# A two-layer encoder on one core: matmul operands and tiles moved to other places in SBUF, modulo 512 bytes

## The chip, the core and the metric

The kernel runs on one core of one Trainium2 chip. The metric is the device time in microseconds (us) of the whole program; the time before is the median of three runs. Everything is float32; products are taken as three matmuls on halves (see below), so the work of TensorE (PE) is three times that of the plain products.

## The reference, cut to what matters

512 tokens of width 1024 pass through two layers. Layer 0 mixes by stick-breaking attention, layer 1 by a gated linear recurrence (RG-LRU); each is followed by an MLP with squared ReLU, and a last norm ends it.

```
x = x + stick_breaking_attention(rms_norm(x, norm_mix[0]), w_qkv, w_o)
u = relu(rms_norm(x, norm_mlp[0]) @ mlp_w1[0]);  x = x + (u * u) @ mlp_w2[0]
x = x + rglru_block(rms_norm(x, norm_mix[1]), ...)
u = relu(rms_norm(x, norm_mlp[1]) @ mlp_w1[1]);  x = x + (u * u) @ mlp_w2[1]
return rms_norm(x, norm_final)
```

## The kernel before

**Halves.** Each float32 operand is split into a high half that PE reads as fp32r and a low half that is the rest. ScalarE (ACT) writes the high half with a copy, VectorE (DVE) the low one with a subtraction. A product takes three matmuls: high by high, high by low, low by high (`three`, L219 to L221; `up`, L966; `times`, L1061). x lies in `xgh` and `xgl`, a second pair of activations in `bh` and `bl`, the weights in `wh` and `wl`, of which `wpool` holds four pairs of 4 KB per partition, and in the RG stage `wmore` two more.

**A matmul has two operands in SBUF.** The stationary one (128 columns, 512 bytes per partition) is loaded ahead of the matmul (the profile's PEld rows), the moving one (512, 384, 256 or 128 columns) streams through. All rows of a tile that a matmul reads start a multiple of 512 bytes from the tile's start, so the distance between the two operands' starts, modulo 512, is fixed by where the tiles start.

**Stages in order of time.** Attention with its projections and output product to about 250 us; the first quarter of the MLP's up-projection ("m1", `Mlp.squared`, L219 to L221, 512 columns) to 294.9; layer 0's MLP to 564; the RG block with its output product to about 715; m1 of layer 1 to 763.8; layer 1's MLP to the end.

**The MLP** (`Mlp.run`, L1061 and L966) takes the rest as Strassen-like seven-product schemes (`PRODUCTS`): "up" passes with two units of seven steps, 24 matmuls of 256 columns each (x's blocks moving, weights stationary), and "down" passes with 14 steps, 12 matmuls of 512 columns each (the weights moving, the blocks of u stationary: `bh`, `bl` for unit 0, `sh`, `sl` for unit 1). In up, products P1, P2 and P4 read `xgh` and `xgl`; P5 and P3 read the tile `s41` with `low`; P6 reads a corner of `bh` or `bl` with `low`; P7 reads `xgh` with `low`. Each layer has four down passes and three up passes between them. The order of a down pass stands in `ORDERS`; "mid" is P1 0, P5 0, P1 1, P2 0, P5 1, P6 0, P6 1, P3 0, P3 1, P7 0, P7 1, P2 1, P4 0, P4 1, where the digit is the unit.

**What sets the order.** PE's instructions are in written order. Within `Mlp.run` those of DVE and ACT are too (`Ordered`): `leave(i)` runs when step i is written, evacuates its PSUM bank, and prepares the weights of step i + 4 (`operand`: ACT copies `wh`, then DVE writes `wl`), for which the pair of step i has to be free. Sums of weight blocks are added by DVE (`b<-b,b`) or by DMAs that accumulate (POOL's queue).

**Places.** Tiles of a pool lie one behind the other in the order in which they are first asked for, and pools lie one behind the other in the order in which they are opened; so whatever is put ahead of a tile, or lengthens one, moves all that is placed behind it.

Of the kernel before, what the change touches and what calls it, by code (L numbers as in the profile page):

```python
# [11 lines left out]
F32 = mybir.dt.float32  # L12
F32R = mybir.dt.float32r
AF = mybir.ActivationFunctionType
# [3 lines left out]
P = 128  # L18
S = 512
D = 1024  # L20
C = D // P
# [3 lines left out]
EPS = 1e-6  # L25
RG_C = 8.0
SCALE = HD ** -0.5


START = [  # L30
# [31 lines left out]
def hybrid_encoder(  # L62
# [24 lines left out]
    V, A, G, PE = nc.vector, nc.scalar, nc.gpsimd, nc.tensor  # L87

    const = ctx.enter_context(tc.tile_pool(name="const", bufs=1))
# [13 lines left out]
    def f(ap):  # L103
        return ap.bitcast(F32)


    colt = const.tile([P, cols.shape[1]], F32, tag="colt", name="colt")

    def col(name):
        o, n = COLS[name]  # L110
        return colt[:, o : o + n]
# [4 lines left out]
    make_identity(nc, ident)  # L116
    eps_t = const.tile([P, 1], F32, tag="eps", name="eps_t")
    V.memset(eps_t, EPS)

    xgh = const.tile([P, C, S], F32R, tag="xgh", name="xgh")  # L120
    xgl = const.tile([P, C, S], F32R, tag="xgl", name="xgl")
    bh = const.tile([P, C, S], F32R, tag="bh", name="bh")
    bl = const.tile([P, C, S], F32R, tag="bl", name="bl")

# [1 line left out]
    def halves(gname, c, xc):  # L126

        g = col(gname)[:, c : c + 1]
        A.activation(xgh[:, c, :], xc, AF.Identity, scale=g)
        return V.scalar_tensor_tensor(  # L130
            xgl[:, c, :], xc, g, f(xgh[:, c, :]), ALU.mult, ALU.subtract
        )
# [90 lines left out]
    def dense(src, ah, al, tag=None, halves=None, ks=range(C), ps=None):  # L223

        wh, wl = halves or slab(src, ks=ks)
        ps = bank(tag) if ps is None else ps
        for k in ks:
            three(ps, ah[:, k, :], al[:, k, :], wh[:, k, :], wl[:, k, :], k == ks[0], k == ks[-1])
        return ps

    def beside(ws, ah, al, pss, at, ks=range(C)):
# [8 lines left out]
    ctx.enter_context(tc.manual_schedule(engines={mybir.EngineType.PE}))  # L240


    lams = {
        n: const.tile([P, C], F32, tag=f"lam_{n}", name=n)
        for n in ("ab", "pp", "den", "s1", "s2", "pl", "c8", "c4")
    }
    c8, c4 = lams["c8"], lams["c4"]

    def softplus():

        ab, pp, den, s1, s2, pl, _, _ = lams.values()
        lam = col("lam")

        sigmoid = yield
        V.tensor_scalar(ab, lam, -1.0, None, ALU.mult)
        V.tensor_tensor(ab, ab, lam, ALU.max)
        with tc.issue_after(sigmoid.ins):
            A.activation(pp, ab, AF.Sigmoid, scale=-1.0)
        with tc.issue_after((yield).ins):
            V.tensor_scalar(den, pp, -1.0, 2.0, ALU.mult, ALU.add)  # L260
        V.reciprocal(den, den)
        V.tensor_tensor(s1, pp, den, ALU.mult)
        V.tensor_tensor(s2, s1, s1, ALU.mult)
        V.tensor_scalar(pl, s2, 1.0 / 17, 1.0 / 15, ALU.mult, ALU.add)
        for n in (13, 11, 9, 7, 5, 3, 1):
            V.tensor_tensor(pl, pl, s2, ALU.mult)
            V.tensor_scalar(pl, pl, 1.0 / n, None, ALU.add)
        V.tensor_tensor(pl, pl, s1, ALU.mult)
        V.tensor_scalar(den, lam, -1.0, 0.0, ALU.mult, ALU.max)
        V.scalar_tensor_tensor(c8, pl, 2.0, den, ALU.mult, ALU.add)  # L270
        V.tensor_scalar(c4, c8, RG_C * 0.5, None, ALU.mult)
        V.tensor_scalar(c8, c8, -RG_C, None, ALU.mult)
        yield
# [5 lines left out]
    NB = S // P  # L279
    PAIRS = H // 2  # L280
    half = [slice(0, HD), slice(HD, P)]
    so, early = {}, {}
# [4 lines left out]
    def home_tile(tag, n, name):  # L287
        return home.tile([P, S], F32, tag=tag, name=name, bufs=n)

    with ExitStack() as actx:  # L290
        hp = actx.enter_context(tc.tile_pool(name="hp", bufs=2))
        sp = actx.enter_context(tc.tile_pool(name="sp", bufs=1))


        later = sp.tile([P, S], F32, tag="later", name="later")
        G.memset(later, 0.0)
        G.affine_select(
# [11 lines left out]
        for i in range(2):  # L309
            both = []  # L310
            for nm in ("h", "l"):
                t = sp.tile([P, 2 * P], F32R, tag=f"last{nm}{i}", name=f"last{nm}{i}")
                G.memset(f(t[:, :P]), 0.0)
                both.append(t)
            lasts.append(both)
# [117 lines left out]
        def inverse():  # L433
# [9 lines left out]
            with tc.high_priority():  # L443
                norm["root"] = A.activation(rc, pc[:, :NB], AF.Sqrt, bias=eps_t, scale=1.0 / D)
                V.reciprocal(rc, rc)
                for t in range(NB):
                    ts = slice(t * P, (t + 1) * P)
                    V.tensor_scalar(diag[:, ts], ident, rc[:, t : t + 1], None, ALU.mult)
                V.tensor_scalar(rp, rc, SCALE, None, ALU.mult)
                V.tensor_scalar(rn, rc, -SCALE, None, ALU.mult)  # L450
            norm.update(rc=rc, rp=rp, rn=rn)
# [280 lines left out]
    def add_x(c, ps):  # L732
        V.tensor_tensor(x[c], x[c], ps, ALU.add)

    def residual(srcs, gname, begun={}, ready={}):

        for c in range(C):
            add_x(c, begun[c][0] if c in begun else dense(srcs[c], bh, bl, halves=ready.get(c)))
            halves(gname, c, x[c])

    residual(w_so, "mlp0", so, so_next)


# [23 lines left out]
    class Mlp:  # L767
# [28 lines left out]
        def __init__(self, ctx, layer):  # L796
            self.layer, self.sq, self.first = layer, Squares(), None
            self.V, self.A = Ordered(V), Ordered(A)
            self.mp = ctx.enter_context(tc.tile_pool(name=f"mlp{layer}", bufs=2))
            self.c = [  # L800
                self.mp.tile([P, 2, S], F32, tag=f"c{i}", name=f"c{i}", bufs=1) for i in range(4)
            ]
            self.begun, self.a = set(), {}
            self.turns = count()
            self.blocks = ExitStack()
            self.bp = self.blocks.enter_context(tc.tile_pool(name=f"blocks{layer}", bufs=2))
            self.u, self.lows, self.s3, self.slots = {}, {}, [], None

            self.s41 = self.bp.tile([P, C // 2, S], F32R, tag="s41", name="s41", bufs=1)

        def y(self, t, h):

# [500 lines left out]
    with ExitStack() as mctx:  # L1313
        mlp = Mlp(mctx, 0)

        dram = mctx.enter_context(tc.tile_pool(name="dram", bufs=1, space=bass.MemoryType.DRAM))
        away = dram.tile([P, C, S], F32, tag="away", name="away")
        squares = Squares()
        last = {}

        def feature(c, tag):

            pt = bank(tag)
            for t in range(NB):
                PE.transpose(
                    pt[:, t * P : (t + 1) * P], mlp.y(t, c // 4)[:, c % 4 * P : (c % 4 + 1) * P],
                    ident,
                )
            add_x(c, pt)
            last["low"] = halves("mix1", c, x[c])  # L1330

        def end(ws, xs):
            for i in range(2):
                for g in range(2):
                    mlp.times("P4", g, i, ws[g], xs[i], False)
                mlp.collect("P4", i, xs[i])
                if i == 0:
                    for c in range(4, C):
                        feature(c, "zzoo"[c - 4])
                        squares.chunk(c, x[c], e=G)  # L1340

        def between(c):
            nc.sync.dma_start(out=away[:, c, :], in_=x[c])
            if c == C - 1:
                soft.send(mlp.ready)

        def back():
            for c in range(C):
                x[c] = home_tile(*HOMES[c], "x")
                nc.sync.dma_start(out=x[c], in_=away[:, c, :])  # L1350

        end.ready = back
        mlp.quarters(between, end)

        begin = [bank("acc") for _ in range(2)]
        beside(
            [slab(w_in[C + i]) for i in range(2)], xgh, xgl, begin,
            {
                1: lambda: [feature(c, "z") for c in range(2)],
                2: lambda: [feature(c, "o") for c in range(2, 4)],  # L1360
            },
            (*range(4, C), *range(4)),
        )
        behind[0] = last["low"].ins
        third = slab(w_in[C + 2])
        behind[0] = None
        sq = squares
        with tc.tile_pool(name="squares", bufs=4) as pool:
            for c in range(4):
                sq.chunk(c, x[c], last["low"], pool)  # L1370

    wctx = ExitStack()

    wmore = wctx.enter_context(tc.tile_pool(name="wmore", bufs=2))


    with ExitStack() as rctx:
# [196 lines left out]
        for k in range(C):  # L1574
            for c in range(4):
                ps, wh, wl = begun[c]
                three(ps, bh[:, k, :], bl[:, k, :], wh[:, k, :], wl[:, k, :], k == 0, k == C - 1)

    residual(w_ro, "mlp1", begun, {4: ws["o4"]})
    wctx.close()  # L1580


    with ExitStack() as mctx:
        lp = mctx.enter_context(tc.tile_pool(name="last", bufs=1))
        mlp = Mlp(mctx, 1)

        def between(c):
# [20 lines left out]
                )  # L1608


        A.activation(lp.tile([P, 1], F32, tag="rt", name="early"), eps_t, AF.Sqrt)

        ss = lp.tile([P, NB, 3], F32, tag="ss", name="ss")
        bias = lp.tile([P, NB], F32, tag="bias", name="bias")

        def square(t, h, i, cols=slice(0, S), end=False):

# [129 lines left out]
```

## Time and profile before

| what | value |
|---|---|
| time, median of 3 runs | 1049.12 us (1048.78 to 1049.46) |
| span of the profiled execution | 1047.9 us; the median lies 1.2 us above it |
| PE matmul busy | 1035.1 us, 99% of the span, 5868 matmuls |
| DVE, ACT, POOL busy | 863.1 (82%), 701.5 (67%), 179.2 (17%) us |
| DMA | 159.41 MB, mean 152 GB/s |

The profile is of one execution. Matmuls are pipelined: a row's own length (0.28 us for 256 columns) is longer than the time until the next one starts. What a matmul costs is therefore read from start to start, or from a piece of the chain of work that counts them (24 in 2.88 us). "Idle before <-releaser" in a row is how long the engine stood still ahead of it, and what ended that. Steps are named by their product (P1 to P7) and unit, as above.

### The profile page before, as it was taken

The page shows a single profiled execution, that of the slowest core. Times are in us where ns is not written, and L with a number is a line of the kernel's source. Part 1 is how long each engine was busy: PE and PEld are TensorE (multiplying, and loading weights), DVE is VectorE, ACT ScalarE, POOL GpSimd, SP SyncE. Part 2 cuts the span into 40 slices and gives each one's busy share as a digit, 9 for nine tenths or more (in the row PEclk, how much of TensorE's full clock was granted, in tenths as well). Part 3 has the DMA queues.
Part 4 walks back from the last instruction along what each step waited for, and adds up shares of the span by engine and source line. Part 5 has one row for each costly group of instructions (what it writes and reads, how often), then busy time and mean ns, then how long its engine had stood idle before and what let it go on. Part 6 is the DMA issues. An engine that isn't in the chain of part 4 may idle for free.

```text
span 1047.9 us, 15859 instructions
## 1 busy us (share of the span) xinstructions
PE 1035.1 (99%) x5868; PEld 902.8 (86%) x5868; DVE 863.1 (82%) x1147; ACT 701.5 (67%) x1082; POOL 179.2 (17%) x238
## 2 busy tenths in 40 slices
PE   8999999999999999999999999999999999999997
PEld 7888888888888988988988788888888988988986
DVE  7888787848788898898899799984789797897897
ACT  6767676836766773773775699964755773773775
POOL 2344344420000010010011121200000010010013
PEclk9999999999999999999999999999999999999999
DMA  6745354537536667567582483352345667567553
GB/s 225 204 137 141 101 149 104 153 109 274 149 80 190 181 139 204 165 140 207 164 208 81 109 214 112 91 221 93 88 86 173 174 142 206 158 139 204 145 125 101
DMA packets 52828, 159.41 MB, mean 152 GB/s; under 512 B 6672, under 2 KB 7952, under 8 KB 52752
## 3 DMA queue, kind: packets, MB, share of 16 engines
q1 hardware_dynamic: 41808, 120.13, 34.4%
q0 software_dynamic: 10368, 37.75, 20.9%
q8 instruction: 46, 0.75, 0.3%
q10 hardware_dynamic: 576, 0.52, 0.2%
q14 instruction: 30, 0.25, 0.1%
HBM read 137.41 MB, written 4.19 MB: 135 GB/s over the span
## 4 chain that ended last, share of the span: by engine, by line
PE 88%; DVE 5%; ACT 3%; issue 2%; DMA 2%; ACTq 0%; POOL 0%; DVEq 0%; POOLq 0%
PE ps_t L1061 14%; PE ps_acc L966 8%; PE ps_z L966 8%; PE ps_acc L1061 7%; PE ps_acc L219 5%; PE ps_acc L221 5%; PE ps_acc L220 5%; PE ps_o L966 5%; PE ps_z L1061 4%; PE ps_o L219 2%; PE ps_t L220 2%; PE ps_o L220 2%; PE ps_o L221 2%; PE ps_t L221 2%; PE ps_t L219 2%
## 5 line engine op out<-in xcount | busy, mean ns | idle before, releaser
L757 ACT CAST wh<-b 128x1024 fp32r<-128x1024 f32 x168 | 174.0, 1047 | 125.6 <-DVE b L757 76.7
L757 DVE TENSOR_TENSOR wl<-b,wh 128x1024 fp32r<-128x1024 f32 x168 | 203.8, 1221 | 50.5 <-ACT wh L757 50.1
L1043 POOL DMA_DIRECT2D b<-in_w_dn x40 | 35.0, 875 | 360.9 <-DVE b L757 204.6
L219 PE MATMUL ps_acc<-xgh,wh 128*128 128x512 f32 x192 | 78.5, 409 | 0.0
L221 PE MATMUL ps_acc<-xgl,wh 128*128 128x512 f32 x192 | 75.2, 392 | 0.0
L220 PE MATMUL ps_acc<-xgh,wl 128*128 128x512 f32 x192 | 75.1, 391 | 0.0
L581 DVE TENSOR_TENSOR_SCAN scan<-keep,later 128x128 f32<-128x128 f32 (+1 forms) x64 | 59.6, 933 | 18.8 <-ACT keep L571 10.9
L214 DVE TENSOR_TENSOR wl<-raw,wh 128x512 fp32r<-128x512 f32 (+2 forms) x70 | 60.9, 895 | 16.2 <-ACT wh L212 16.1
L757 ACT ACTIVATE u<-u 128x512 f32<-128x512 f32 x100 | 63.1, 632 | 6.5 <-DVE u L757 4.8
L212 ACT CAST wh<-raw 128x512 fp32r<-128x512 f32 (+2 forms) x70 | 50.8, 759 | 23.1 <-PE ps_acc L221 7.3
L1043 POOL DMA_DIRECT2D b<-in_w_up x24 | 20.8, 867 | 240.5 <-DVE b L757 72.1
L585 POOL TENSOR_TENSOR w<-w,scan 128x128 f32<-128x128 f32 (+1 forms) x64 | 51.9, 813 | 55.9 <-DVE scan L581 53.2
L757 DVE TENSOR_TENSOR b<-b,b 128x1024 f32<-128x1024 f32 x48 | 58.7, 1224 | 1.3
L757 DVE TENSOR_TENSOR u<-u 128x512 f32<-128x512 f32 (+1 forms) x92 | 54.9, 596 | 2.7 <-ACT u L757 1.1
L966 PE MATMUL ps_z<-xgh,wh 128*128 128x256 f32 x192 | 54.2, 282 | 0.0
L966 PE MATMUL ps_z<-xgh,wl 128*128 128x256 f32 x192 | 54.1, 282 | 0.0
L757 ACT CAST wh<-raw 128x1024 fp32r<-128x1024 f32 x46 | 47.9, 1045 | 9.3 <-PE ps_acc L1061 8.4
L966 PE MATMUL ps_acc<-low,wh 128*128 128x256 f32 x192 | 53.6, 279 | 0.0
L1061 PE MATMUL ps_t<-wl,sh 128*128 128x512 f32 x126 | 50.1, 398 | 0.0
L1061 PE MATMUL ps_t<-wh,sh 128*128 128x512 f32 x126 | 49.6, 394 | 0.0
L1061 PE MATMUL ps_t<-wh,sl 128*128 128x512 f32 x126 | 49.4, 392 | 0.0
L1061 PE MATMUL ps_t<-wh,bh 128*128 128x512 f32 x126 | 49.2, 391 | 0.0
(399 smaller groups left out, 3434.4 us busy)
## 6 DMA issues: line engine op xcount, KB each, us to landing
b<-in_w_dn SPq DMA_DIRECT2D x48, 512.0 KB, 4.5
b<-in_w_dn POOLq DMA_DIRECT2D x40, 512.0 KB, 5.5
b<-in_w_up SPq DMA_DIRECT2D x36, 512.0 KB, 4.6
b<-in_w_up POOLq DMA_DIRECT2D x24, 512.0 KB, 5.3
raw<-in_w_m SPq DMA_DIRECT2D x16, 512.0 KB, 4.1
raw<-in_w_dn SPq DMA_DIRECT2D x16, 512.0 KB, 4.7
raw<-in_w_in SPq DMA_DIRECT2D x16, 512.0 KB, 4.2
raw<-in_w_qk SPq DMA_DIRECT2D x12, 512.0 KB, 3.7
```

The source lines that it names most:

```text
L212: A.copy(wh[:, k, :], raw[:, k, :])
L214: V.tensor_tensor(wl[:, k, :], raw[:, k, :], f(wh[:, k, :]), ALU.subtract)
L219: PE.matmul(ps, wh, ah, start=start, stop=False)
L220: PE.matmul(ps, wl, ah, start=False, stop=False)
L221: PE.matmul(ps, wh, al, start=False, stop=stop)
L581: V.tensor_tensor_scan(sc[:, S - n : S][:, ::-1], keep[:, :n][:, ::-1], later[:, S - n :][:, ::-1], 1.0, ALU.mult, ALU.max,)
L585: G.tensor_tensor(wt, wt, sc[:, S - n + 1 : S + 1], ALU.mult)
L757: ins = getattr(self.e, name)(*args, **kwargs)
L966: PE.matmul(ps[:, i * HS : (i + 1) * HS], m, y, start=new and i == k == n == 0, stop=i == 1 and k == C // 2 - 1 and n == 2, skip_group_che ...
L1043: G.dma_start(out=unit[b].rearrange("p j n -> p (j n)"), in_=unit["src"](to), accum_op=ALU.add)
L1061: PE.matmul(ps, m, y[:, jj, cols], start=first and n == 0, stop=last and n == 2, skip_group_check=not new,)
```

## The change

It moves tiles, and nothing else: on every engine the same instructions stand in the same order as before, on tiles of the same contents. `xgh` and `xgl` get 64 bytes more each (`ASIDE`, 16 elements), and `x_at` chooses whether x starts at the tile's start or 64 bytes behind it: 64 behind in attention and the RG block, at the start from the residual sum ahead of each MLP on. `s41` gets 64 bytes more in layer 0 and 192 more in layer 1 (`APART`). A few small tiles are placed earlier (`lams`, `colt`, `ss`, `bias`, the four `last` tiles of attention), two are only there to fill ("apart"), and one, a scalar that only preloads ACT's table of square roots, now goes to a corner of the MLP's tile `c[0]`.

```diff
+ASIDE = 16
+APART = (16, 48)
...
-    xgh = const.tile([P, C, S], F32R, tag="xgh", name="xgh")
-    xgl = const.tile([P, C, S], F32R, tag="xgl", name="xgl")
+    xgh_t = const.tile([P, C * S + ASIDE], F32R, tag="xgh", name="xgh")
+    colt = const.tile([P, cols.shape[1]], F32, tag="colt", name="colt")
+    ss = const.tile([P, S // P, 3], F32, tag="ss", name="ss")
+    xgl_t = const.tile([P, C * S + ASIDE], F32R, tag="xgl", name="xgl")
+    const.tile([P, 4 * ASIDE], F32, tag="apart", name="apart")
+    def x_at(aside):
+        nonlocal xgh, xgl
+        xgh, xgl = (
+            t[:, aside : aside + C * S].rearrange("p (c s) -> p c s", s=S) for t in (xgh_t, xgl_t)
+        )
+    x_at(ASIDE)
...
+    x_at(0)
     residual(w_so, "mlp0", so, so_next)
...
-            self.s41 = self.bp.tile([P, C // 2, S], F32R, tag="s41", name="s41", bufs=1)
+            t = self.bp.tile([P, C // 2 * S + APART[layer]], F32R, tag="s41", name="s41", bufs=1)
+            self.s41 = t[:, : C // 2 * S].rearrange("p (k s) -> p k s", s=S)
...
         def end(ws, xs):
+            x_at(ASIDE)
...
+    wmore.tile([P, ASIDE], F32, tag="apart", name="apart", bufs=1)
...
+    x_at(0)
     residual(w_ro, "mlp1", begun, {4: ws["o4"]})
...
-        lp = mctx.enter_context(tc.tile_pool(name="last", bufs=1))
-        A.activation(lp.tile([P, 1], F32, tag="rt", name="early"), eps_t, AF.Sqrt)
+        A.activation(mlp.c[0][:, 0, :1], eps_t, AF.Sqrt)
```

By the addresses of the two built programs, the tiles start at these bytes modulo 512, before and after: `xgh`, `xgl` 32 and 448 (with `x_at(ASIDE)` 0); `bh`, `bl` 32 and 256; `wh`, `wl` in `wpool` 288 and 256, in `wmore` 480 and 0; `s41` 480 in layer 0 and 96 in layer 1, now 448 in both; `sh`, `sl` 480 and 96, now 0 and 128; `low` 480 and 448. The distance from the stationary operand's start to the moving one's, modulo 512, follows:

| products (line) | operands | matmuls | columns | before | after |
|---|---|---|---|---|---|
| projections of attention and of RG | x with weights | 1056 | 512, 256 | 256 | 256 |
| four products of RG, weights in wmore | x with weights | 96 | 512 | 64 | 0 |
| m1, both layers (L219 to L221) | x with weights | 384 | 512 | 256 | 192 |
| output products w_so, w_ro | bh, bl with weights | 294 | 512 | 256 | 0 |
| output products and gates, other weights | bh, bl with weights | 138 | 512 | 64 | 256 or 320 |
| up P1, P2, P4, and xgh in P7 (L966) | x with weights | 1056 | 256 | 256 | 192 |
| up P5, P3, layer 0 / layer 1 | s41 with weights | 192 / 192 | 256 | 192 / 320 | 192 |
| up, low parts of P3, P5, P6, P7 | low with weights | 384 | 256 | 192 (24: 320) | 192 |
| up P6, corner | bh, bl with weights | 192 | 256 | 256 | 0 |
| down, unit 0 (L1061) | weights with bh, bl | 666 | 512 | 256 | 0 |
| down, unit 1, layer 0 / layer 1 | weights with sh, sl | 336 / 330 | 512 | 320 / 192 | 256 / 128 |
| scores and values of attention | q, k and w, v | 224 | 512 to 256 | 0 | 0 |
| its last value product | last with v | 32 | 256 | 96 | 0 |
| transposes | identity with a tile | 224 | 128 | 32 | 192 |

No instruction moves, so no order is set against another one. The one row that reads otherwise is ACT's, at the end of the RG block, where `early` was written; `Activation`, `PE`, `Pool`, and `DMASW` name what an instruction waits for. ACT before:

```order
L129 ACTIVATE xgh<-x,colt 128x512 [waits DVE_49]
L151 ACTIVATE ssq<-x 128x512
L1611 ACTIVATE early<-eps_t 128x1 [waits DMASW5_49,DMASW6_49,DMASW0_49,PE_49]
L129 ACTIVATE xgh<-x,colt 128x512 [waits DVE_49]
L154 ACTIVATE sq<-x 128x512
```

ACT with the change:

```order
L148 ACTIVATE xgh<-x,colt 128x512 [waits DVE_49]
L170 ACTIVATE ssq<-x 128x512
L1633 ACTIVATE c_7345<-eps_t 128x1 [waits DMASW0_49,DMASW5_49,PE_49,DMASW6_49,Activation_49,Pool_49]
L148 ACTIVATE xgh<-x,colt 128x512 [waits DVE_49]
L173 ACTIVATE sq<-x 128x512
```

The place is the same. The instruction now also waits for POOL's last sum of the RG block (`aa`, L1530) and ACT's last write of `bh` there, since `c[0]` takes their memory over. An evacuation of m1 that waited for that POOL sum before does so no more. No other wait differs.

More of the change, by code (lines that the diff above doesn't have):

```diff
@@ L104, in f @@
         return ap.bitcast(F32)
-    colt = const.tile([P, cols.shape[1]], F32, tag="colt", name="colt")
     def col(name):
@@ L118, in hybrid_encoder @@
     V.memset(eps_t, EPS)
-    xgh = const.tile([P, C, S], F32R, tag="xgh", name="xgh")
-    xgl = const.tile([P, C, S], F32R, tag="xgl", name="xgl")
+    bias = const.tile([P, S // P], F32, tag="bias", name="bias")
+    lams = {
+        n: const.tile([P, C], F32, tag=f"lam_{n}", name=n)
+        for n in ("ab", "pp", "den", "s1", "s2", "pl", "c8", "c4")
+    }
+    c8, c4 = lams["c8"], lams["c4"]
+    xgh_t = const.tile([P, C * S + ASIDE], F32R, tag="xgh", name="xgh")
[3 more added lines that the diff above has]
+    const.tile([P, 4 * ASIDE], F32, tag="apart", name="apart")
+    xgh = xgl = None
+    def x_at(aside):
[4 more added lines that the diff above has]
+    x_at(ASIDE)
     bh = const.tile([P, C, S], F32R, tag="bh", name="bh")
@@ L240, in hybrid_encoder @@
     ctx.enter_context(tc.manual_schedule(engines={mybir.EngineType.PE}))
[L243 to L247, printed above, removed]
     def softplus():
@@ L292, in hybrid_encoder @@
         sp = actx.enter_context(tc.tile_pool(name="sp", bufs=1))
+        last_of = {
+            (nm, i): sp.tile([P, 2 * P], F32R, tag=f"last{nm}{i}", name=f"last{nm}{i}")
+            for i in range(2) for nm in "hl"
+        }
         later = sp.tile([P, S], F32, tag="later", name="later")
@@ L311, in hybrid_encoder @@
             for nm in ("h", "l"):
-                t = sp.tile([P, 2 * P], F32R, tag=f"last{nm}{i}", name=f"last{nm}{i}")
+                t = last_of[nm, i]
                 G.memset(f(t[:, :P]), 0.0)
@@ L1608, in factors @@
                 )
-        A.activation(lp.tile([P, 1], F32, tag="rt", name="early"), eps_t, AF.Sqrt)
-        ss = lp.tile([P, NB, 3], F32, tag="ss", name="ss")
-        bias = lp.tile([P, NB], F32, tag="bias", name="bias")
+        A.activation(mlp.c[0][:, 0, :1], eps_t, AF.Sqrt)
         def square(t, h, i, cols=slice(0, S), end=False):
```

## The prediction

> **What bounds the kernel now.** I read the page first, then the chain of work, then the stages.
>
> ```profile
> PE 1035.1 (99%) x5868; PEld 902.8 (86%) x5868; DVE 863.1 (82%) x1147; ACT 701.5 (67%) x1082; POOL 179.2 (17%) x238
> PE 88%; DVE 5%; ACT 3%; issue 2%; DMA 2%; ACTq 0%; POOL 0%; DVEq 0%; POOLq 0%
> ```
>
> PE is never out of work, and 88% of the chain that ended last is PE. The change lets PE wait for nothing new, so the question is what one matmul costs from start to start. The chain of work through layer 0's second up pass (unit 1) and third down pass has start, length and number of matmuls in each row:
>
> ```profile
> 431.25 2.88 PE ps_z L966 x24
> 434.12 2.74 PE ps_o L966 x24
> 436.86 2.83 PE ps_z L966 x24
> 439.69 2.72 PE ps_o L966 x24
> 442.41 2.83 PE ps_z L966 x24
> 445.24 2.86 PE ps_o L966 x24
> 448.10 2.88 PE ps_z L966 x24
> ...
> 453.73 2.72 PE ps_acc L1061 x12
> 456.44 2.75 PE ps_t L1061 x12
> ```
>
> The seven steps are P1, P5, P6, P3, P7, P2, P4: equal matmuls of 256 columns, none with a wait. Where every operand lies at distance 192 (P5, P3) 24 take 2.73; where x lies at 256 (P1, P4) 2.88; mixed steps (P6, P7) lie between. The last two rows are down steps: blocks at 256 take 2.72, `sh` at 320 takes 2.75. Layer 1, first P5 and then a down step of unit 1:
>
> ```profile
> 905.99 2.83 PE ps_o L966 x24
> ```
> ```profile
> 849.72 2.80 PE ps_t L1061 x12
> ```
>
> The same P5 costs 2.83 at distance 320 instead of 192. With 512 columns it is the other way round: `sh` at 192 is the dearest, 2.80. So the distance does set the rate; the gain is 5% with 256 columns, and 192 is the wrong place with 512.
>
> [...]
>
> **The change part by part.** PE's own sum first, at those rates.
>
> Up: P1, P2 and P4 go from 2.88, 2.86, 2.88 to 2.73 (-0.43 a unit), P7 from 2.83 to 2.73 (-0.10); in layer 1 also P5 and P3 (-0.10 each). P6's corner goes from 256 to 0, taken as equal (its 2.83 could become 2.73 or 2.88). Two units, three passes: -3.2 in layer 0, -4.4 in layer 1, -7.6 us together.
>
> M1 goes the other way, from 256 to 192 with 512 columns. One m1 product, and one RG product at distance 64, from first matmul to the next product's first (the count includes that one):
>
> ```profile
> 272.14:277.58 5.44, 5.44 (x25) 1.00 0.09 36
> 633.39:638.88 5.49, 5.49 (x25) 1.00 0.00 0
> ```
>
> 24 matmuls take 5.44 at 256. At 192 the row of `sh` gives 2 x 2.80 = 5.60. M1 has 16 products: +2.6 us. No row shows x moving at 192 with 512 columns, so the bounds are 0 and 2.6, or a little beyond; I take 2.6, since `sh` is at that distance in a steady run.
>
> Down, unit 1: layer 0 from 320 to 256, 28 steps by 2.75 - 2.72: -0.8. Layer 1 from 192 to 128, which no row shows. By distance 128 lies halfway between 64 (5.49 / 2 = 2.75) and 192 (2.80): I take 2.77, 27.5 steps, -0.8. Bounds: 2.72 (-2.2), and 2.85 (+1.4) if it is worse than 192 by as much as 192 is than 64. Nothing below 2.72 is to be had: 2.72 / (12 x 512) is 0.443 ns a column and 2.73 / (24 x 256) 0.444, so both shapes have the same floor.
>
> Down, unit 0, and the output products go from 256 to 0: 666 and 294 matmuls, 80 steps of 12. Distance 0 stands only in attention, in pairs:
>
> ```profile
> 151.32 0.40 PE L629 MATMUL ps_o<-th,v 128*128 128x512 f32 x1
> ...
> 151.79 0.39 PE L219 MATMUL ps_acc<-xgh,wh 128*128 128x512 f32 x1
> ...
> 152.48 0.34 PE L562 MATMUL ps_z<-kh,q 128*128 128x384 f32 x1
> ```
>
> Two matmuls at 0 take 0.47 (0.235 each), the three at 256 behind them 0.69 (0.230), both dearer than the steady 0.227, so a pair just after another shape says little. Distances 64 and 320 cost the same (5.49 / 2 and 2.75), which suggests that it counts modulo 256 and that 0 is 256. I take 2.72; bounds 2.72, the floor, and 2.80 (0 to +6.4 us of PE).
>
> RG products from 64 to 0, output products and gates from 64 to 256: -0.3. Transposes move from 32 to 192, for which no row exists; taken as 0, 1 us either way by the 5% above on some 24 us.
>
> PE's sum: -7.6 + 2.6 - 0.8 - 0.8 - 0.3 = **-6.9 us**. But PE is not alone at the end of the line.
>
> **The second chain.** Where down pass 3 reaches its seventh step (P6 1), PE stops for DVE. First the chain's rows on both sides, then the timeline's rows of the weight load and of DVE:
>
> ```profile
> 464.66 5.66 PE ps_t L1061 x24
> 470.32 5.48 PE ps_acc L1061 x24
> ```
> ```profile
> 466.22 2.36 DVE L757 TENSOR_TENSOR wl<-b,wh 128x1024 fp32r<-128x1024 f32 x2 [0.57 <-ACT wh L757]
> ```
> ```profile
> 467.50 0.19 PEld L1061 LDWEIGHTS ps_t<-wl,sh 128*128 128x128 f32 x1 [0.32 <-DVE wl L757]
> ```
>
> PE loses 5.66 - 5.48 = 0.18 us there: DVE's `wl` (the first of the two) ends at 467.45, and the load starts at 467.50. What DVE waits for in the 45 us ahead of it, and where that begins on ACT:
>
> ```profile
> DVE wl L757 <- ACT wh L757: 2.9, 6, 0.6
> DVE bl L757 <- ACT bh L757: 1.5, 1, 1.5
> DVE sl L757 <- ACT sh L757: 0.6, 1, 0.6
> DVE u L757 <- ACT u L757: 0.2, 1, 0.2
> ```
> ```profile
> 422.71 1.05 ACT L757 CAST wh<-b 128x1024 fp32r<-128x1024 f32 x1 [1.19 <-PE ps_acc L966]
> ```
> ```profile
> 422.70:467.50 44.80, 44.80 (x313) 41.64 (x312) 39.86 (x45) 33.62 (x45) 5.21 (x6) 1.00 0.64 153
> ```
>
> DVE works 39.9 of 44.8 us (third pair of the last row) and waits the rest for ACT alone, never for PE. Step by step back from 467.45, each row starts where a DVE or ACT row ends, until ACT's `wh` at 422.71, which waited for the end of the up pass's fourth step (its weight pair came free). So from the fourth up step to the seventh down step **two chains run side by side and end within 0.2 us**. The work of DVE and ACT does not depend on this change. PE's gain between 422.7 and 467.5 (ten of fourteen up steps) only makes the wait longer. It is kept only from 467.5 to the next fourth up step, at 500.7.
>
> What is kept, layer 0: in the first pass, from a like stop at 303.4 to the fourth up step's end at 344.8, six steps of unit 1 by 0.03 and one P1 by 0.15, -0.33; 389.6 to 422.7 and 467.5 to 500.7, five steps and one P1 each, -0.6; 545.5 to the end of the pass, -0.15. Together -1.1 of -4.0.
>
> Layer 1, its waits of weight loads in the MLPs, and the reserve of DVE's `wl` (start, length; the first of two) at the seventh step of the third down pass and the tenth of the last one:
>
> ```profile
> PEld ps_t L1061 <- DVE wl L757: 1.2, 4, 0.3
> PEld ps_z L966 <- ACT u L757: 1.2, 1, 1.2
> ```
> ```profile
> 938.08 2.36 DVE L757 TENSOR_TENSOR wl<-b,wh 128x1024 fp32r<-128x1024 f32 x2 [0.57 <-ACT wh L757]
> ```
> ```profile
> 1024.63 2.35 DVE L757 TENSOR_TENSOR wl<-b,wh 128x1024 fp32r<-128x1024 f32 x2
> ```
> ```profile
> 939.69 0.39 PE L1061 MATMUL ps_t<-wl,sh 128*128 128x512 f32 x1
> ```
> ```profile
> 1026.72 0.39 PE L1061 MATMUL ps_acc<-wl,sh 128*128 128x512 f32 x1
> ```
>
> The wait of 1.2 us is in layer 1's first up pass, at 829.7: ACT and DVE are the later chain there too, and up to 860.9 only about -0.4 is kept. 860.9 to 894.5 is PE's: five steps of unit 1, P1, P5 and P3, -0.48. Then the chain, which ends at 938.08 + 1.22 = 939.30 against PE's 939.69: -0.33 is to be had. 939.7 to 973: -0.48. Then the chain ends at 1024.63 + 1.22 = 1025.85 against 1026.72: -0.8 is to be had. Together -2.5 of -5.2.
>
> M1 (+2.6) and the RG products (-0.3) lie on PE's own path and count in full.
>
> ACT's scalar that now goes to `c[0]` waits for two more things:
>
> ```profile
> 693.74 0.19 ACT L1611 ACTIVATE early<-eps_t 128x1 f32<-128x1 f32 x1
> ```
> ```profile
> 681.51 0.92 POOL L1530 TENSOR_SCALAR aa<-d 128x512 f32<-128x512 f32 x1 [8.59 <-DVE d L757]
> ```
>
> POOL's sum is over 11 us earlier, and ACT's own write stands ahead of it in its queue: 0. Were POOL late, ACT's `xgh` behind it, and with it m1's first matmul, would wait as long.
>
> Sum: 2.6 - 0.3 - 1.1 - 2.5 = **-1.3 us**. The profiled span is 1047.9, 1.2 below the median of the runs; taken off the median: 1049.1 - 1.3 = **1047.8 us**.
>
> **The rivals.** *All of PE's sum is kept*: 1049.1 - 6.9 = 1042.2. For it: the page gives PE 88% of the chain. Against it: DVE's rows above. 9%.
>
> *M1 costs nothing more*, because x moving at 192 settles otherwise than weights over `sh`: -1.3 - 2.6, 1045.2. The rows of `sh` speak against it, but they come from other tiles. 17%.
>
> *Distance 0 is dear with 512 columns* (slower): a matmul whose two operands start at the same place modulo 512 pays what `sh` pays at 192, 2.80 instead of 2.72 a step. The output products (24.5 steps) and some 25 unit-0 steps on PE's own stretches count, 50 x 0.08 = +4.0: 1051.8. It decides from 0.026 a step, where it eats the 1.3. For it: the pairs of attention; against it: 64 equals 320. 15%.
>
> *The distance is not the cause*: P5's 2.74 and 2.83 differ by layer, and what I put down to distance belongs to something that does not move. Then 1049.1. Against it: P1 costs 2.88 in both layers, so the layer itself changes nothing. 12%.
>
> **How the numbers follow.** Forecast 47%, own range 1046.6 to 1049.6 by the bounds of distance 128 and of P6. The range from 1045.2 to 1051.8 takes in all but the full gain, some of m1's case, and what lies past the dear 0. Faster by over 0.2% (2.1 us, about what a measurement of this kernel can tell from no change): the full gain, most of m1's case and a little of the forecast, 30%. Slower by over 0.2%: most of the dear 0, 12%. Within: 58%.
>
> **What would show it.** Up steps of 2.73 everywhere but P6; m1 products of 5.60; unit-0 steps of 2.72; unit-1 steps of 2.72 in layer 0 and 2.77 in layer 1. PE's wait at the seventh down step grows from 0.18 to about 1 us in layer 0, with DVE's and ACT's rows unchanged. I am wrong if the waits do not grow (then more is kept), if m1 stays at 5.44, or if unit-0 steps take 2.80.

## The result, and the profile after

The changed kernel takes 1051.46 us (median of 9 runs, 1049.42 to 1052.27), the kernel before beside it 1048.78 (1048.18 to 1049.92): a ratio of 1.0017, 95% interval 1.0008 to 1.0027, so it is slower, by 0.8 to 2.8 us. The same kernel measured again, on another occasion (`after_again` below), gave 1.0007 (0.9996 to 1.0018). Both agree with a loss of 0.8 to 1.9 us. The forecast was a gain of 1.3.

The page's rows of busy time and of the chain that ended last, after the change:

```profile
PE 1034.5 (98%) x5868; PEld 898.7 (86%) x5868; DVE 863.5 (82%) x1147; ACT 701.2 (67%) x1082; POOL 177.1 (17%) x238
PE 78%; DVE 9%; ACT 5%; DMA 4%; issue 3%; SPq 0%; POOL 0%; ACTq 0%; DVEq 0%; POOLq 0%
```

PE's share of the chain fell from 88% to 78%, and DVE's and ACT's rose from 8% to 14%: the second chain of the prediction has come forward. Second profiles of both kernels say the same (PE 90% before, 80% after). Where the time went is read from stages. The rows below are stretches from one matmul's start to another's, the same matmuls in both kernels; the columns are the stretch and its length, then busy time and instructions of PE, PEld, DVE, ACT and POOL, PE's granted clock, and DMA. In order: m1 of layer 0, layer 0's MLP, the RG block's middle with its output product, m1 of layer 1, and layer 1's MLP from its second down pass to its last. Before:

```profile
249.93:294.86 44.93, 44.93 (x204) 37.32 (x202) 36.89 (x59) 29.31 (x45) 1.89 (x2) 1.00 0.61 200
294.86:564.65 269.79, 269.79 (x1671) 242.06 (x1669) 236.50 (x284) 175.06 (x224) 26.08 (x30) 1.00 0.64 166
...
620.00:715.03 95.03, 95.03 (x420) 78.47 (x418) 82.03 (x115) 79.29 (x110) 14.22 (x11) 1.00 0.46 144
715.03:763.80 48.77, 48.58 (x234) 40.37 (x233) 28.76 (x46) 29.50 (x47) 1.78 (x2) 1.00 0.29 77
...
844.09:1039.99 195.90, 195.90 (x1186) 174.51 (x1185) 170.73 (x191) 123.11 (x168) 26.00 (x26) 1.00 0.62 151
```

After:

```profile
251.56:297.70 46.14, 46.14 (x204) 37.21 (x202) 37.14 (x59) 29.35 (x45) 1.89 (x2) 1.00 0.60 194
297.70:567.49 269.79, 269.69 (x1670) 242.36 (x1669) 236.38 (x284) 175.24 (x224) 26.11 (x30) 1.00 0.66 166
...
623.13:717.88 94.75, 94.75 (x420) 78.47 (x418) 82.75 (x115) 79.28 (x110) 9.91 (x11) 1.00 0.46 144
717.88:767.69 49.81, 49.64 (x234) 40.37 (x233) 28.92 (x46) 29.47 (x47) 1.78 (x2) 1.00 0.29 76
...
848.08:1042.32 194.24, 193.90 (x1186) 171.16 (x1185) 170.71 (x191) 123.02 (x168) 26.68 (x26) 1.00 0.63 152
```

M1 costs 1.21 + 1.04 = 2.25 more, the RG block 0.28 less, layer 1 1.66 less, and **layer 0's MLP gives nothing at all**. The sum is +0.3. The span grew by 2.4 (1047.9 to 1050.3; the profiled execution after is the slowest of its nine runs); the rest stands in stretches in which two profiles of one and the same kernel differ as much. The stretch up to m1 took 250.43 here and 248.92 in the second profile of the changed kernel. The first stretch of the RG block and the first up pass of layer 1 moved by more than 1 us between two profiles of the kernel before (`before_again`).

Why layer 0 gives nothing is seen in three up steps of 24 matmuls, P7, P2 and P4 of unit 0, where x is moving. Before, in layer 0 and in layer 1:

```profile
422.51:431.08 8.57, 8.57 (x74) 8.57 (x73) 7.03 (x9) 6.12 (x9) 0.86 (x1) 1.00 0.71 188
...
894.37:902.95 8.58, 8.58 (x75) 8.58 (x73) 7.01 (x9) 6.14 (x9) 0.88 (x1) 1.00 0.72 187
```

After, the same steps:

```profile
425.39:433.87 8.48, 8.48 (x74) 8.48 (x73) 6.96 (x8) 6.03 (x9) 0.86 (x1) 1.00 0.72 190
...
898.05:906.21 8.16, 8.16 (x74) 8.16 (x73) 7.00 (x8) 5.72 (x8) 0.88 (x1) 1.00 0.68 193
```

These are the same tiles at the same addresses in both layers, at distance 192, and no PE wait and no drop of the clock (1.00) in either row: 8.16 / 3 = 2.72 in layer 1 as forecast, and 8.48 / 3 = 2.83 in layer 0. P5 and P3 of layer 0, which did not change their distance at all, became dearer, from 2.74 and 2.72 to 2.83. From the chain of work after the change, P5 of unit 1 (2.74 before) and then two down steps, unit 0 and unit 1:

```profile
436.86 2.83 PE ps_o L986 x24
...
453.82 2.72 PE ps_t L1081 x12
456.54 2.72 PE ps_acc L1081 x12
```

So at one distance, 192, two rates were measured, 2.72 and 2.83. What differs inside is seen in the groups of weight loads of those two stretches. The rows are line, operation, shapes and count, then busy us and mean ns of one. Layer 0, and then layer 1:

```profile
L986 PEld LDWEIGHTS ps_acc<-xgl,wh 128*128 128x128 f32 x8 | 1.5, 192 | 0.0
```
```profile
L986 PEld LDWEIGHTS ps_acc<-xgl,wh 128*128 128x128 f32 x8 | 1.5, 188 | 0.0
```

In layer 0 every third load takes 192 ns instead of 188, in a pattern that repeats from product to product; in layer 1 none does.

### The profile page after: what moved, and what is told of

The parts are those of the page before. It is cut to its first block, busy times and chain, and to the rows that moved or that the text cites. A ratio compares the mean times of both kernels' runs of the same rounds, so it can differ in the third digit from the quotient of the medians.

```text
span 1050.3 us, 15859 instructions
## 1 busy us (share of the span) xinstructions
PE 1034.5 (98%) x5868; PEld 898.7 (86%) x5868; DVE 863.5 (82%) x1147; ACT 701.2 (67%) x1082; POOL 177.1 (17%) x238
## 4 chain that ended last, share of the span: by engine, by line
PE 78%; DVE 9%; ACT 5%; DMA 4%; issue 3%; SPq 0%; POOL 0%; ACTq 0%; DVEq 0%; POOLq 0%
PE ps_t L1081 13%; PE ps_acc L986 7%; PE ps_acc L1081 7%; PE ps_z L986 6%; PE ps_acc L238 4%; PE ps_acc L240 4%; PE ps_acc L239 4%; PE ps_o L986 3%; PE ps_z L1081 3%; DVE wl L776 3%; PE ps_t L239 2%; PE ps_t L240 2%; PE ps_t L238 2%; PE ps_o L238 2%; PE ps_o L240 2%
```

## The experiments

**The changed kernel again**, without an edit.

> The changed kernel itself once more. In its first profile the up steps of layer 0 take 2.83 us per 24 matmuls and those of layer 1 take 2.72, although every operand lies at the same distance, 192, in both. Theory R (there are two steady rhythms at this distance, and what runs on PE just ahead picks one; the program fixes it): the same again, 2.83 in layer 0, 2.72 in layer 1 outside the steps behind a long stop; time 1049.4 to 1052.3. Rival N (each execution falls into either by chance): some of the passes change sides, and the time follows, by 1 to 2 us. The attention stage, where the changed kernel's first profile lost 1.6 us at three waits of PE for DVE (near 24, 41 and 117 us): if that is scatter between executions, this profile shows less or more of it; if the new places cause it, the same 1.6.

1050.17 us against 1049.20; ratio 1.0007 (0.9996 to 1.0018). P7, P2 and P4 of unit 0 in layer 0's second up pass, and in layer 1's first and second one:

```profile
423.86:432.34 8.48, 8.48 (x74) 8.48 (x73) 6.96 (x8) 6.03 (x9) 0.86 (x1) 1.00 0.75 190
...
815.74:824.22 8.48, 8.48 (x74) 8.48 (x73) 6.44 (x7) 5.95 (x8) 0.86 (x1) 1.00 0.60 194
...
895.69:903.85 8.16, 8.16 (x75) 8.16 (x73) 6.99 (x8) 5.71 (x8) 0.89 (x1) 1.00 0.70 191
```

P7, P2 and P4 repeat to 0.01 in all six units of layer 0 (8.48) and in all four of layer 1's second and third pass (8.16). In layer 1's first pass, which has two stops of PE for ACT (0.3 and 2.3 in the first profile), the units changed places: unit 0 was at 8.16 and unit 1 at 8.48 in the first profile, and here they are at 8.48 and 8.16. So between these two profiles the rate changed in the pass with these stops alone: rival N holds only behind a stop. Attention took 1.5 us less than in the first profile, so what it lost there was scatter.

**One number: the blocks of layer 0 at 128.**

```diff
-APART = (16, 48)
+APART = (48, 48)
```

> One number changed: in layer 0 the blocks sh and sl of unit 1 stand at distance 128 from the weights, as in layer 1 (256 in the changed kernel). Theory R (two rhythms at 192; the down steps ahead pick): unit-1 down steps of layer 0 go from 2.72 to about 2.80 us per 12, and the up steps of layer 0 settle in the fast rhythm, 2.72 instead of 2.83 per 24, though nothing of the up steps moved; PE gains about 3 x 13 x 0.11 = 4.3 and loses 28 x 0.08 = 2.2 us in layer 0, most of it between the waits for DVE, whose length then changes; time 1049 to 1052. Rival L (something else of layer 0, such as the traffic of the other engines, sets 2.83): up steps stay at 2.83, down steps are dearer by 2.2 in sum, and the time is up to 2.2 above the changed kernel's, 1052 to 1053.6.

1051.10 us, 1.0016 (1.0005 to 1.0028). Two half steps of unit 1 in layer 0's third down pass, and P7, P2, P4 of unit 0 in the second up pass, which reads nothing that moved:

```profile
456.76:459.55 2.79, 2.79 (x13) 2.26 (x12) 2.57 (x4) 2.79 (x5) 0.82 (x1) 1.00 0.73 115
```
```profile
423.63:431.79 8.16, 8.16 (x75) 8.16 (x73) 6.99 (x8) 5.72 (x8) 0.86 (x1) 1.00 0.74 192
```

Theory R is right and L is wrong: the down steps became dearer (2.72 to 2.79), and the up steps of layer 0, whose tiles lie where they lay, fell from 8.48 to 8.16 or 8.17 in five of the six units. The sixth, unit 1 of the first pass, stayed at 8.48, and so did unit 1 of layer 1's second pass, which is as in the changed kernel here and took 8.16 in both profiles of that kernel:

```profile
365.18:373.66 8.48, 8.48 (x74) 8.48 (x73) 8.45 (x10) 6.63 (x10) 0.86 (x1) 1.00 0.57 187
...
913.91:922.39 8.48, 8.48 (x74) 8.48 (x73) 8.45 (x10) 6.62 (x10) 0.86 (x1) 1.00 0.59 185
```

Both stand behind a stop of PE for ACT at P6 of the same unit; the profile has six such waits (2.5 us in sum, 1.1 the longest), the changed kernel's three. In layer 1's second pass the changed kernel stops there too (0.3) and took 8.16 behind it, so what comes out behind a stop is not fixed by the place. Yet the layer as a whole became dearer, since the gain is not kept. The stage row of layer 0's MLP, and the weight load that stops PE at the seventh step of the third down pass:

```profile
295.57:566.12 270.55, 269.95 (x1671) 239.14 (x1669) 236.23 (x284) 175.40 (x224) 26.08 (x30) 1.00 0.66 166
```
```profile
468.63 0.19 PEld L1081 LDWEIGHTS ps_t<-wl,sh 128*128 128x128 f32 x1 [0.61 <-DVE wl L776]
```

The same load waited 0.46 in the changed kernel and 0.32 before: PE waits longer for DVE there.

**One number: the blocks of layer 1 at 256.**

```diff
-APART = (16, 48)
+APART = (16, 16)
```

> One number changed: in layer 1 the blocks sh and sl of unit 1 stand at distance 256 from the weights, as in layer 0 (128 in the changed kernel). Theory R: unit-1 down steps of layer 1 go from 2.80 to 2.72 per 12 and the up steps of layer 1 fall into the slow rhythm, 2.83 instead of 2.72 per 24, though nothing of them moved; PE loses about 3 x 13 x 0.1 = 3.9 and gains 27 x 0.08 = 2.2; time 1050.5 to 1053. Rival L (something of the layer itself): up steps stay at 2.72 and the down steps' gain comes on top, 1049 to 1051.

1050.20 us, 1.0007 (0.9996 to 1.0018). A unit-1 down step of layer 1, and P7, P2, P4 of unit 0 in its second up pass:

```profile
930.26:932.98 2.72, 2.72 (x13) 2.25 (x12) 2.69 (x4) 2.72 (x4) 0.27 (x1) 1.00 0.77 96
```
```profile
896.55:905.03 8.48, 8.48 (x74) 8.48 (x73) 6.96 (x8) 6.03 (x9) 0.88 (x1) 1.00 0.73 192
```

The mirror image: the down step fell from 2.79 to 2.72, and the up steps, unmoved, rose from 8.16 to 8.47 or 8.48 in the second and third pass; in the first, whose stretch has PE busy for 77.60 of 80.10 us, they took 8.16. The time is 0.3 below the range expected: from the second down pass on, layer 1 takes 194.44 (194.24 and 194.68 in the changed kernel's two profiles), so the down passes gain about as much as the up passes lose.

**One extra matmul ahead of each up pass**, on the kernel with `APART = (16, 16)`.

```diff
+KICK = {(0, 1): 32, (0, 2): 64, (0, 3): 96, (1, 1): 128, (1, 2): 160, (1, 3): 192}
...
+                    if kick and i == k == 0:
+                        PE.matmul(
+                            ps[:, :kick], wh, h[:, :kick], start=True, stop=True,
+                            skip_group_check=True,
+                        )
```

> The kernel with sh at 256 in both layers, in which every up step but those behind a stop runs at 2.83, and ahead of the first matmul of each up pass one more matmul, on the same operands, of 32, 64, 96 columns in layer 0's passes and 128, 160, 192 in layer 1's (its result is overwritten by the next one). No tile moves. Theory R (the moment at which a run is entered picks the rhythm): in at least one of the six passes the steps behind the extra matmul run at 2.72 per 24 and stay there for several steps, in others at 2.83; nothing in between lasts. Rival L (place alone, or the kind of step ahead, sets the rate): all steps stay at 2.83. Time: 1049 to 1051, some 0.05 us per extra matmul, and up to 1 us less per pass that changes sides.

1049.65 us, 1.0003 (0.9993 to 1.0013). P7, P2, P4 of unit 0 in the six passes, in order:

```profile
347.31:355.79 8.48, 8.48 (x75) 8.48 (x73) 7.16 (x8) 6.04 (x9) 0.88 (x1) 1.00 0.76 194
...
425.10:433.25 8.15, 8.15 (x74) 8.15 (x73) 6.99 (x8) 5.72 (x8) 0.86 (x1) 1.00 0.73 193
...
502.93:511.09 8.16, 8.16 (x75) 8.16 (x73) 6.99 (x8) 5.73 (x8) 0.86 (x1) 1.00 0.74 195
...
816.80:825.28 8.48, 8.48 (x74) 8.48 (x73) 6.34 (x7) 5.95 (x8) 0.86 (x1) 1.00 0.67 201
...
896.93:905.41 8.48, 8.48 (x74) 8.48 (x73) 6.96 (x8) 6.03 (x9) 0.88 (x1) 1.00 0.72 186
...
974.72:982.88 8.16, 8.16 (x74) 8.16 (x73) 6.99 (x8) 5.72 (x8) 0.86 (x1) 1.00 0.73 197
```

Widths of 64, 96 and 192 columns bring unit 0 of the pass into the fast rhythm, 32, 128 and 160 don't; the fourth row is of layer 1's first pass, where the changed kernel has its two stops, and says less. In the sixth pass unit 1 is slow again (8.48); the changed kernel stops there for 0.3 at P6. No tile moved, and the steps that these rows time come four steps behind the extra matmul. So it is shown for this kernel that **what PE does at the entry** picks the rhythm, with every operand in its place (in `l1_256`, without the extra matmuls, the three fast rows stood at 8.48), and that it then held for the 72 matmuls of these rows. An extra matmul as such is not enough, since those of 32 and 160 columns changed nothing (8.48). That it is the moment of entry fits, but each width stood in one pass only, and what makes the two rhythms is not shown.

**Without the move of x.**

```diff
-    x_at(0)
+    x_at(ASIDE)
     residual(w_so, "mlp0", so, so_next)
...
-    x_at(0)
+    x_at(ASIDE)
     residual(w_ro, "mlp1", begun, {4: ws["o4"]})
```

> The changed kernel without the move of x: x stays at distance 256 from the weights in the MLPs too; s41, low, the blocks and all else lie as in the changed kernel. Both m1 products go back from 5.60 to 5.44 us each, 16 of them: -2.6 us on PE's own path. Up P1, P2 and P4 go to 2.87, P5 and P3 to 2.73 (theory R: the long run at 256 ahead of them brings them into the fast rhythm, in layer 0 and in layer 1). Time 1048 to 1050, near the kernel before. Rival (the loss of the changed kernel comes from elsewhere, such as attention): 1050.5 to 1052.

1048.13 us, 0.9983 (0.9973 to 0.9994): 2 us below the changed kernel on the same chip, and faster than the kernel before. M1 of layer 0 and of layer 1:

```profile
248.40:293.33 44.93, 44.93 (x204) 37.32 (x203) 36.88 (x59) 29.39 (x45) 1.89 (x2) 1.00 0.65 199
...
712.28:761.04 48.76, 48.56 (x234) 40.38 (x233) 28.76 (x46) 29.49 (x47) 1.78 (x2) 1.00 0.31 77
```

Both are back to the values before, to 0.01, though x and the weights start at other places than before (0 and 256 instead of 32 and 288, modulo 512): what counts here is the distance, not the place of either tile. Unit 1's P5 in layer 1's second pass, which took 2.83 before with `s41` at 320, runs at 2.74 behind a long run at distance 256, as theory R had it:

```profile
902.79:905.53 2.74, 2.74 (x26) 2.74 (x25) 2.40 (x2) 2.31 (x4) 0.00 (x0) 1.00 0.84 139
```

P1 ahead of it reads x at 256 in both kernels. So the place of an operand does count for 256 columns too, beside the entry.

**M1 with an extra matmul**: is its price at 192 a rhythm too?

```diff
+KICK = (32, 64, 96, 128, 160, 192), (48, 80, 112, 144, 176, 224)
...
+        if kick:
+            PE.matmul(
+                ps[:, :kick], wh[:, 0, :], ah[:, 0, :kick], start=True, stop=True,
+                skip_group_check=True,
+            )
```

> The changed kernel with one extra matmul ahead of the first of each m1 product but the first two of a layer (its result is overwritten): of 32, 64, 96, 128, 160 and 192 columns in layer 0, of 48, 80, 112, 144, 176 and 224 in layer 1. Theory R extended to 512 columns (m1's price at distance 192 is a slow rhythm too): in some of the twelve products 24 matmuls go back from about 5.60 to 5.44 us and m1 gets up to 1.8 us cheaper in sum. Rival S (with 512 columns and distance 192 there is only the one rate): all twelve stay at 5.6, and the time is that of the changed kernel plus 12 extra matmuls of about 0.05 us.

1050.34 us, 1.0014 (1.0004 to 1.0023). The 24 matmuls of one product behind extra ones of 32 and of 128 columns in layer 0, and of 224 in layer 1:

```profile
261.59:267.27 5.68, 5.68 (x26) 4.60 (x25) 4.23 (x5) 4.43 (x7) 0.00 (x0) 1.00 0.79 282
...
278.74:284.38 5.64, 5.64 (x26) 4.57 (x25) 4.45 (x8) 4.63 (x7) 1.20 (x2) 1.00 0.70 108
...
760.85:766.46 5.61, 5.61 (x25) 4.53 (x25) 4.34 (x12) 2.19 (x4) 0.00 (x0) 1.00 0.00 0
```

The twelve take 5.61 to 5.69; none falls below 5.60. Rival S is right for every entry tried: with 512 columns and distance 192 no product came back to 5.44. In the changed kernel itself the products behind smaller matmuls take 5.67 to 5.69, with 314 to 320 ns from the first start to the second. In the last product of each layer the starts behind that stand about 231 and 236 ns apart in turn, where most products have 233 and 234 throughout; the two patterns have the same mean, 233.

**Less work for DVE, with the change and without it.** Half of each `wl` of the Strassen-like passes is left out, and PE reads `wh` again in its place.

```diff
-                    wh, wl = (t[:, k, i * P : (i + 1) * P] for t in w)
+                    wh, wl = (t[:, k, i * P : (i + 1) * P] for t in (w[0], w[k < C // 4]))
...
-            self.V.tensor_tensor(wl, raw, f(wh), ALU.subtract)
+            self.V.tensor_tensor(wl[:, :1], raw[:, :1], f(wh[:, :1]), ALU.subtract)
...
-                for n, (m, y) in enumerate(((h, wh), (h, wl), (l, wh))):
+                for n, (m, y) in enumerate(((h, wh), (h, (wl, wh)[jj]), (l, wh))):
```

> The changed kernel with half of DVE's work on the low halves of the weights of the Strassen-like passes left out (128x512 instead of 128x1024 per step; PE reads the high half again in the place of what is missing, so it has as much to do): to be set against the same edit of the kernel before. Theory C (PE's gain is lost at waits for DVE and ACT): with DVE some 6 us lighter in each window of 45 us these waits go in both kernels, and what is left between the two is PE's own sum: m1 +2.25, RG -0.3, layer 0 about -0.1, layer 1's up steps up to -4.5 where they find the fast rhythm: this one 0.5 to 3 us faster than the other light kernel. Rival D (the gain is lost on PE itself): 0.5 to 1 us slower than the other light kernel, as without the edit.

> The kernel before with the same edit as the other light kernel: half of DVE's work on the low halves of the weights left out, PE's work as it was. Its waits of PE for DVE and ACT inside the MLPs go too, which are 1.2 at the longest and 0.2 us at each seventh step of a down pass: 1.5 to 2.5 us faster than the kernel before, 1046.5 to 1047.5. Theory C: 0.5 to 3 us slower than the changed light kernel. Rival D: 0.5 to 1 us faster than it.

1044.31 us with the change (4 runs, 1044.04 to 1044.70) and 1046.73 without it (10 runs, 1045.97 to 1048.56): relieved of the waits, **the change gains 2.4 us** by the medians, and the two sets of runs do not overlap. Layer 0's MLP and layer 1's from the second down pass on, with the change:

```profile
296.60:565.09 268.49, 268.49 (x1671) 242.70 (x1670) 191.72 (x284) 174.22 (x224) 26.10 (x30) 1.00 0.67 167
...
841.66:1034.26 192.60, 192.60 (x1187) 171.53 (x1186) 138.32 (x189) 121.36 (x166) 23.89 (x26) 1.00 0.64 154
```

And without it:

```profile
294.85:563.76 268.91, 268.91 (x1670) 242.35 (x1669) 192.34 (x284) 174.05 (x224) 26.09 (x30) 1.00 0.66 167
...
840.21:1036.00 195.79, 195.79 (x1186) 174.59 (x1185) 138.46 (x189) 121.01 (x165) 23.74 (x25) 1.00 0.63 151
```

In layer 1 PE's own gain in this stretch is 195.79 - 192.60 = 3.19, of which the full kernels kept 1.66 (195.90 to 194.24), and 1.22 in the second profile (194.68): about half, or less. In layer 0 the own gain is 0.42. Theory C holds for layer 1; in layer 0, where the changed kernel's up steps take 2.83, there was only 0.42 to lose.

**The kernel before again.**

> The kernel before once more, for a second profile: its up and down steps should take what they took (2.88, 2.74, 2.83, 2.72 in layer 0), since nothing in it moved, and the attention stage shows how far two executions of one kernel differ there (between two profiles of the changed kernel it was 1.1 us).

Its P7, P2 and P4 take 8.56 to 8.58 wherever no stop falls into them. The stretches that scatter are the first of the RG block and layer 1's MLP up to its second down pass:

```profile
564.65:618.72 54.07, 54.06 (x253) 44.28 (x251) 47.22 (x66) 42.43 (x62) 10.86 (x11) 1.00 0.55 145
...
762.48:843.99 81.51, 79.49 (x505) 71.49 (x504) 69.89 (x83) 52.19 (x68) 6.92 (x8) 1.00 0.58 150
```

In the first profile of the same kernel they took 55.35 and 80.29, so a difference of 1.2 or 1.3 us in either says nothing about a change. The attention stage agreed to 0.05 here (248.76 against 248.81), less scatter than between the two profiles of the changed kernel.

**What beats both.** Two undone parts together: x at 256 and the blocks of layer 1 at 256.

```diff
-APART = (16, 48)
+APART = (16, 16)
...
-    x_at(0)
+    x_at(ASIDE)
```

> Two undone parts together: x at 256 in the MLPs, and sh of layer 1 at 256 (128 in the changed kernel). From the stage table: m1 -2.25, layer 1's four down passes -1.2 against the changed kernel, its up passes as in x_256 (-0.9 against the kernel before). If the parts add up: 1046.5 to 1047.5, 2 us below the kernel before. If the second chain takes the down passes' gain back: 1048 to 1048.5, as x_256 alone.

1045.98 us against 1049.03; 0.9974 (0.9964 to 0.9984), 3 us faster than the kernel before and 0.5 below the range expected, so the parts add up. Layer 1's MLP from the second down pass:

```profile
841.40:1034.96 193.56, 193.50 (x1186) 173.52 (x1185) 170.54 (x191) 122.85 (x168) 26.56 (x26) 1.00 0.64 153
```

That is 2.34 less than before (195.90), with x at 256, where P1 took 2.88 before. I put the gain down to the unit-1 down steps (2.80 before, 2.72 in `l1_256`), to the unit-0 steps, most of which took 2.75 before, and to P5 and P3 at 192 (P5 at 2.83 before, at 2.74 in `x_256`).

## Why the prediction failed, step by step

**The rate belongs to the distance** ("where every operand lies at distance 192 (P5, P3) 24 take 2.73"): this step failed. The rows were right, but they came from P5 behind P1 at 256 and from P3 behind P6, and I read them as a property of the place. At 192 the runs show two steady rhythms, 2.72 and 2.83, and the entry picks one: behind down steps at 0 and 256 the slow one, behind steps at 128 the fast one. `l0_128`, `l1_256` and `kick` show it, each without moving an operand of the steps that change. In layer 0 the up passes even lost 0.1 each, since P5 and P3 fell into the slow rhythm too. The term of -1.1 for layer 0 came out at 0, the largest part of the miss. Distance does belong to the rate, as P5 in `x_256` shows; what the prediction left out is the entry.

The prediction's two P5 rows (2.74 and 2.83) were therefore no proof that place matters, because the same work at the same place also gives 2.72 and 2.83. What shows that the distance is not indifferent is m1, 46.14 in the changed kernel and 44.93 with x's place alone undone, and the down steps, 2.72 and 2.79 with that of `sh` and `sl` alone. What makes one distance dearer than another, no run shows.

**M1**: right in kind, +2.25 instead of +2.6. A product in the middle takes 5.60 as forecast; the stage's rows have 1.21 and 1.04 for eight products each instead of 1.3, since those next to other matmuls or a stop (the last of layer 0, seven of layer 1) grew by 0.09 to 0.15 instead of 0.16. The rival that m1 costs nothing more is out. The product that took 5.44 at 272.14, after the change:

```profile
274.41:280.01 5.60, 5.60 (x25) 4.49 (x24) 4.27 (x5) 2.90 (x4) 0.53 (x1) 1.00 0.05 21
```

**Distance 0 as good as 256**: right. Unit-0 steps without a stop took 2.72 in layer 0, all but the first, and 2.73 to 2.78 in layer 1 (2.72 to 2.75 before); the rival of a dear 0, which had them at 2.80, is out. Where layer 1's were above 2.72, unit-1 steps at another distance lay between them: in `l0_128` one of layer 0's, unmoved, took 2.76 between them too (from 465.07 to 467.83 by its weight loads), against 2.72 in the changed kernel. **Unit 1 in layer 0**: right (2.75 to 2.72). **Unit 1 in layer 1**: 2.79 to 2.80 instead of the 2.77 taken; inside the bounds, and no gain where 0.8 was booked. **RG products**: -0.28, as forecast.

**The second chain**: right in kind, and a little stronger than forecast. In layer 1 from the stop at 860.9 on, the starts of the same matmuls show -0.42, -0.22, -0.41 and -0.67 for the terms -0.48, -0.33, -0.48 and -0.8: -1.72 of -2.09, and the second profile has -1.71. Up to there I booked -0.4; the same count shows +0.2 in both profiles, but the scatter of that stretch between two profiles of the kernel before is 1.2. One stop was not foreseen. The fast steps reach P6 of unit 1 before ACT has emptied its bank. The waits of weight loads in layer 1's up passes, after:

```profile
PEld ps_z L986 <- ACT u L776: 2.8, 3, 2.3
```

Before it was one wait of 1.2. The two new ones are in the second and third pass, some 0.25 each. The chain of work there now runs through ACT; it comes to PE at P6 only:

```profile
909.79 0.63 ACT u L776
...
910.43 0.94 ACT wh L776
911.37 0.49 ACT u L776
...
911.90 3.00 PE ps_z L986 x23
```

PE's wait at the seventh down step, which was to grow from 0.18 to about 1 us in layer 0, grew by some 0.13 only, since PE came no earlier.

Put together, with what was measured: +2.25 - 0.28 + 0, and -1.2 to -1.7 for layer 1 by the stage rows of both profiles, gives +0.3 to +0.8 in place of -1.3. The measured loss is 0.8 to 1.9 by what both comparisons allow. That the median of 1051.46 lies next to the 1051.8 of the rival of a dear 0 is chance, since unit-0 steps took 2.72 to 2.78 and not that rival's 2.80. What lies between the account and the measured loss stays open. Attention, whose small tiles moved, can hardly hold much of it: over nine profiles with the changed attention that stretch took from 247.27 to 250.43, 249.0 in the mean, and 248.8 in the three profiles with the old one.

## What to carry to other kernels

A rate read from a steady run held here for the run and its entry, not for the place of its operands alone (2.72 and 2.83 at one place): before a layout is changed for it, look for the same operands at the same distance behind something else, and test with one extra small matmul whether there is a second rhythm. Move one operand at a time and look at every user of it: here x served m1 with 512 columns, where the new place took 5.60 and more for 24 matmuls instead of 5.44, and up with 256, where it took 2.72 or 2.83 instead of 2.88. And where a second chain ends beside PE's (here within 0.2 us), count PE's gain only behind the last wait.

## What was not expected of the hardware

Equal matmuls of 256 columns and their weight loads have, at one and the same distance of their operands (192 modulo 512), two steady rhythms, 112 to 114 and 116 to 119 ns from start to start, at a granted clock of 1.00 in both. An extra matmul of 64, 96 or 192 columns ahead switched one into the other (8.48 to 8.15 or 8.16 for three steps), one of 32 or 160 did not (each tried in one pass), and behind two stops of PE (0.3 and 2.3 us) it changed between two profiles of one kernel. With 512 columns, distance 192 has two patterns as well (233 and 234, or 231 and 236 in turn), but both have a mean of 233 ns, against 227 at distances 0 and 256.
